# A fourth chunk of x turned by VectorE and carried inside SBUF, V's tiles moved by 32 bytes, the last products in fresh banks, four reciprocals put two instructions later

## The chip, the core and the metric

The kernel runs on one core of one Trainium2 chip. The metric is the device time of one execution in microseconds; the time given for the kernel before is the median of 3 runs. Beside the runs there is one profiled execution, whose rows are quoted below. The engines are called as in the profile: PE (TensorE, matrix products), DVE (VectorE), ACT (ScalarE), POOL (GpSimd) and SP (SyncE, which here only issues transfers).

## What is computed

One layer of an encoder trunk on x of 512 tokens by 2048, in float32:

```python
h = rms_norm(x, norm_w)
q, k, v, g_attn, xr, g_lru = jnp.split(h @ w_in, SPLITS, axis=-1)    # widths 1024 256 256 1024 1024 1024
attn_out = attention_group(q, k, v, q_norm_w, k_norm_w)              # 8 heads, 2 key heads, full softmax
lru_out = lru_group(xr, conv_w, conv_b, lru_wa, ...)                 # conv of 4 taps, gated linear scan both ways
mixed = concat([rms_norm(attn_out, attn_norm_w) * silu(g_attn),
                rms_norm(lru_out, lru_norm_w) * silu(g_lru)])
return x + mixed @ w_out                                             # w_out: 2048 by 2048
```

## The kernel before

Every float32 operand of a product is split into a high part (rounded to the PE's float32r format, a cast on ACT) and a low part (the rest, a subtraction on DVE), and each product is done as three: high by high, high by low, low by high. PE thus runs 2755 products, nearly all of 128 stationary columns by 512 moving columns, in an order written out by hand.

**The first stage.** x comes in eight chunks x0 to x7 of 256 columns, one transfer of 512 KB each; `w_in`'s rows come in matching chunks w0 to w7 (`wraw`), and are split by `wsplit` (L218 the cast on ACT, L219 the subtraction on DVE that gives `wl`). The first projection (`proj_feat`, products in L388 and L153 to L155) needs chunk c of x with its columns on the partitions, so x must be turned. Chunks 0 to `TURNED`-1 = 4 are turned on PE: `xturn` runs two times four transposes of 128x128 (L253), after which ACT scales the result by the norm's weight and DVE forms the low part. Chunks 5, 6 and 7 are turned on DVE: `blocks` (L281) transposes 32x32 blocks in place of the whole, `put_aside` (L289) writes the tile to DRAM in one transfer of 512 KB, and `bring_back` (L296) reads it in four transfers of 128 KB that put the blocks where they belong; then ACT scales (L338) and casts (L339) and DVE subtracts (L339). The sums of squares for the norm are formed by `xsquare`, on DVE for the chunks below `TURNED` (L272) and on ACT for the others (L268); their sum (`xsum`, L373) feeds `rstd` on POOL (L346, L347) and two diagonal tiles on DVE (L357 to L360).

The order of these steps is a table, `moves`: after output e of chunk c, the entry (c, e) names the steps that are written next: `x5` is the next step of chunk 5, `w5` the load and `s5` the split of w5. SP's order in this stage is the order written. Each of SP's transfers signals one of eight semaphores in turn, and in the program it waits until the transfer eight places before it has landed. ACT and DVE follow the written order at the start and, from (1, 2) on, an order by priorities that is fixed when the program is built.

**Attention.** `kv` splits the values into `vh` and `vl`, tiles `v` that `values` uses as stationary operand (32 times three products `mm<-ph,v`, `mm<-pl,v`). They are made by `aside`, which takes a tile 64 bytes longer and uses it from byte 32 on. In the built program each of these tiles begins at a multiple of 64 bytes, as the other operands of the products do, so V's data begins at 32 past such a multiple.

**The group norm of the attention.** While the last projection (`C_GA + SEQ`) runs, `later` sums the squares and `spread` gives 1/rms: ACT's square root (L832) and four reciprocals of 128x128 on DVE (L835), whose place among DVE's other work the priorities set.

**The end.** The output product is done with sums of row blocks of `w_out` (seven products in place of eight). In the last group three accumulations are left, and each takes the row pairs i = 6 and 7 at the very end; `last` adds the accumulator (s = 0 and 1 of 128 tokens each) to the output tile on DVE (L1066) and sends it out (L1058). For the last of all, s = 1 is added and sent in two halves of 256 columns.

Of the kernel before, what the change touches and what calls it, by code (L numbers as in the profile page):

```python
# [51 lines left out]
B = 32  # L52
TURNED = 5
NQ = P // B
# [9 lines left out]
def hybrid_kernel(  # L64
# [166 lines left out]
    ssq = const([P, NT, KT // 2], "ssq")  # L231
    highs, x_parts, squared = {}, [], []

# [15 lines left out]
    def xturn(xc, kk, then=None):  # L249
        pt = mm()  # L250
        for t in range(NT):
            ks = slice(kk % 2 * P, (kk % 2 + 1) * P)
            nc.tensor.transpose(pt[:, t * P : (t + 1) * P], xc[:, t, ks], ident)  # L253
# [7 lines left out]
        nc.vector.scalar_tensor_tensor(  # L261
            xl[kk], pt, nw[:, kk : kk + 1], f(xh[kk]), op0=ALU.mult, op1=ALU.subtract
        )

    def xsquare(xc, c):
        for t in range(NT):
            if c >= TURNED:
# [3 lines left out]
                continue  # L271
            square = nc.vector.scalar_tensor_tensor(  # L272
                xc[:, t, :], xc[:, t, :], 1.0, xc[:, t, :], op0=ALU.mult, op1=ALU.mult,
                accum_out=ssq[:, t, c : c + 1],
            )
            if c == 1:
                squared.append(square.ins)

# [13 lines left out]
    def bring_back(to, aside_):  # L292

        src = aside_.rearrange("(i c) b x -> b c i x", c=B)
        for b in range(NQ):
            nc.sync.dma_start(  # L296
                to[b * B : (b + 1) * B].rearrange("p i k t r -> p i (k t r)"), src[b]
            )

    def in_order(v):  # L300
        return v.rearrange("p (t i r) -> p i t r", t=NT, i=NQ)

    def xchunk(c):
# [27 lines left out]
        yield  # L331
        with tc.high_priority(AHEAD), behind(split_done[-1]):
            for k in range(2):
# [4 lines left out]
                nc.scalar.activation(v, v, AF.Identity, scale=nw[:, kk : kk + 1])  # L338
                x_parts[:] = nc.scalar.copy(hi, v).ins, nc.vector.tensor_sub(lo, v, f(hi)).ins  # L339
        yield  # L340

# [312 lines left out]
    def kv(es):  # L654
# [3 lines left out]
        for t in range(NT):  # L658
            vv = es[t][:, NKV * HD :]
            vt = aside(  # L660
                lambda *a: pools["qkv"].tile(*a, tag="v", bufs=NT, name=nm("v")), 2 * NKV * HD // H
            )
            vh[t], vl[t] = vt[:, 0, :], vt[:, 1, :]
# [162 lines left out]

    def spread(dst, parts, n):

# [4 lines left out]
        for t in range(NT):  # L833
            ts_ = slice(t * P, (t + 1) * P)
            nc.vector.reciprocal(dst[:, ts_], dst[:, ts_])  # L835

# [14 lines left out]
    def seven(pair, hi, lo):  # L851
# [11 lines left out]
    def aside(tile_of, n):  # L863

        t = tile_of([P, n * H + 16], F32R)
        return t[:, 8 : 8 + n * H].rearrange("p (n e) -> p n e", e=H)

# [146 lines left out]
    def outputs(work):  # L1014
# [13 lines left out]

        def product(dst, i, k, b, n):
            ah, al = (t[:, k] for t in mixed[i][1])  # L1030
            bh, bl = (t[:, n] for t in b)
            for s in range(2):
                ts_ = slice(s * P, (s + 1) * P)
                for j, (lh, rh) in enumerate(((ah, bh), (ah, bl), (al, bh))):
                    nc.tensor.matmul(  # L1035
                        dst[s], lh[:, ts_], rh, start=i == 0 and j == 0, stop=i == 7 and j == 2
                    )
# [11 lines left out]
        for g in range(2):  # L1049
# [9 lines left out]

            def last(t0, j, acc, cut=1):  # L1060
                for s in range(2):
                    n = cut if s else 1
                    for e0 in range(0, SEQ, SEQ // n):
                        e1 = e0 + SEQ // n
                        to = xs[j][:, t0 + s, e0:e1]
                        nc.vector.tensor_add(to, to, acc[s][:, e0:e1])  # L1066
                        queue = nc.scalar if e1 < SEQ else nc.sync
                        leave(t0 + s, j, queue if g else nc.gpsimd, e0, e1)

# [118 lines left out]
    def split_x(c):  # L1188
# [3 lines left out]
    moves = {  # L1192
# [158 lines left out]
    def later():  # L1351
# [3 lines left out]
        with tc.high_priority():  # L1355
            spread(gbc, parts, NH * HD)
        yield 4
# [88 lines left out]
```

## Time and profile before

| | |
|---|---|
| runs | 630.40, 630.35, 630.19 us; median 630.35 |
| profiled execution | 630.3 us, of which the span of its instructions is 628.2 |
| granted TensorE clock | 0.999 |
| busy | PE 622.0 us, DVE 494.6, ACT 353.1, POOL 101.4 |
| transfers | 127.61 MB, mean 203 GB/s |

Starts are in microseconds from the span's start. A row of the timeline gives start, time taken, engine, line, operation, output<-inputs, shape, the count of instructions put together, and in brackets the idle time of the engine before it and what ended it. A product's row lasts longer than the distance to the next product, since products are pipelined: the pace is read from starts. The chain of work that ended last gives start, share of the time and what it was spent on. A row of transfers gives their number, size and the median time from issue to landing.

### The profile page before, as it was taken

The numbers are of one execution on the slowest core, as the hardware profiler recorded it, in microseconds if no ns is written. First come the engines' busy times: TensorE is split into PE (matmuls) and PEld (weight loads), VectorE is DVE, ScalarE is ACT, GpSimd is POOL, SyncE is SP. The second block draws the span as 40 slices with busy tenths as digits, with TensorE's granted clock in tenths as the row PEclk, the third lists the DMA queues.
The fourth block names the chain that finished last, engine by engine and source line by source line (L and its number), as shares of the span: only waits on it lengthen the run. The fifth ranks groups of instructions, "written<-read, shape, count | busy, mean of one in ns | idle before, by whom it ended". The sixth has DMA issues, their size and how long they took to land.

```text
span 628.2 us, 8273 instructions
## 1 busy us (share of the span) xinstructions
PE 622.0 (99%) x2755; PEld 512.5 (82%) x2755; DVE 494.6 (79%) x794; ACT 353.1 (56%) x618; POOL 101.4 (16%) x134
## 2 busy tenths in 40 slices
PE   9999999999999999999999999999999999999997
PEld 7888888888888888888888888887888888888885
DVE  5958979986699875987887888549978866886885
ACT  3674899379946823555475447438436643444441
POOL 0000210112002622522122232100120101110010
PEclk9999999999999999999999999999999999999999
DMA  8878785859774599479668646922996777896252
GB/s 284 281 209 263 176 202 172 176 134 192 237 234 135 172 255 227 109 214 267 183 170 254 194 150 185 268 69 67 280 232 204 224 254 244 287 340 213 68 201 100
DMA packets 73594, 127.61 MB, mean 203 GB/s; under 512 B 6616, under 2 KB 29264, under 8 KB 73552
## 3 DMA queue, kind: packets, MB, share of 16 engines
q1 hardware_dynamic: 65664, 109.65, 55.9%
q0 software_dynamic: 7712, 17.31, 14.2%
q8 instruction: 21, 0.34, 0.2%
q14 instruction: 21, 0.17, 0.1%
q10 hardware_dynamic: 176, 0.14, 0.1%
HBM read 110.29 MB, written 37.75 MB: 236 GB/s over the span
## 4 chain that ended last, share of the span: by engine, by line
PE 98%; DVE 1%; issue 0%; DVEq 0%; POOL 0%; POOLq 0%
PE pj L155 20%; PE pj L153 20%; PE pj L154 20%; PE mm L1035 14%; PE pj L1035 10%; PE mm L155 4%; PE mm L153 3%; PE mm L154 3%; PE pj L388 1%; PE mm L253 1%; PE mm L1153 1%; DVE gbc L835 1%; DVE wl L219 0%; DVE cb L1066 0%; PE mm L831 0%
## 5 line engine op out<-in xcount | busy, mean ns | idle before, releaser
L155 PE MATMUL pj<-x,wl 128*128 128x512 f32 x376 | 146.8, 390 | 0.4 <-DVE wl L219 0.3
L153 PE MATMUL pj<-x,wh 128*128 128x512 f32 x376 | 147.0, 391 | 0.0
L154 PE MATMUL pj<-x,wh 128*128 128x512 f32 x376 | 146.6, 390 | 0.0
L218 ACT CAST wh<-wr 128x512 fp32r<-128x512 f32 x143 | 85.4, 617 | 81.9 <-PE pj L154 32.0
L219 DVE TENSOR_TENSOR wl<-wr,wh 128x512 fp32r<-128x512 f32 x144 | 100.0, 724 | 21.2 <-ACT wh L218 19.9
L887 ACT CAST wh<-wr 128x1024 fp32r<-128x1024 f32 (+1 forms) x72 | 60.5, 860 | 77.3 <-PE mm L1035 35.9
L888 DVE TENSOR_TENSOR wl<-wr,wh 128x1024 fp32r<-128x1024 f32 (+1 forms) x72 | 68.5, 985 | 30.7 <-ACT wh L887 30.5
L155 PEld LDWEIGHTS pj<-x,wl 128*128 128x128 f32 x376 | 70.6, 188 | 16.1 <-DVE wl L219 1.3
L153 PEld LDWEIGHTS pj<-x,wh 128*128 128x128 f32 x376 | 70.6, 188 | 14.7
L154 PEld LDWEIGHTS pj<-x,wh 128*128 128x128 f32 x376 | 70.6, 188 | 14.7
L153 PE MATMUL pj<-wh,x 128*128 128x512 f32 x192 | 74.8, 389 | 0.0
L155 PE MATMUL pj<-wh,x 128*128 128x512 f32 x192 | 74.8, 389 | 0.0
L154 PE MATMUL pj<-wl,x 128*128 128x512 f32 x192 | 74.8, 389 | 0.0
L911 POOL DMA_DIRECT2D t<-in_w_out_dram x40 | 33.5, 901 | 161.3 <-DMA t<-in_w_out_dram 99.5
L1035 PE MATMUL mm<-wl,mh 128*128 128x512 f32 x128 | 49.8, 389 | 0.0
L1035 PE MATMUL mm<-wh,mh 128*128 128x512 f32 x128 | 49.8, 389 | 0.0
L1035 PE MATMUL mm<-wh,ml 128*128 128x512 f32 x128 | 49.8, 389 | 0.0
L153 PEld LDWEIGHTS pj<-wh,x 128*128 128x128 f32 x192 | 36.0, 188 | 7.5
L154 PEld LDWEIGHTS pj<-wl,x 128*128 128x128 f32 x192 | 36.0, 188 | 7.5
L155 PEld LDWEIGHTS pj<-wh,x 128*128 128x128 f32 x192 | 36.0, 188 | 7.4
L708 POOL TENSOR_SCALAR p<-p,sm 128x512 f32<-128x512 f32 x32 | 24.3, 764 | 90.0 <-DVE sm L707 90.0
L1035 PE MATMUL pj<-wh,mh 128*128 128x512 f32 x96 | 37.4, 390 | 0.0
(200 smaller groups left out, 1038.2 us busy)
## 6 DMA issues: line engine op xcount, KB each, us to landing
wr<-in_w_in_dram SPq DMA_DIRECT2D x71, 512.0 KB, 5.1
wr<-in_w_out_dram SPq DMA_DIRECT2D x24, 512.0 KB, 5.1
t<-in_w_out_dram POOLq DMA_DIRECT2D x40, 256.0 KB, 6.8
wr<-t SPq DMA_DIRECT2D x40, 256.0 KB, 5.9
pd<-u SPq DMA_DIRECT2D x16, 512.0 KB, 3.0
pt<-pd SPq DMA_DIRECT2D x64, 128.0 KB, 3.9
t<-in_w_out_dram SPq DMA_DIRECT2D x24, 256.0 KB, 5.5
t<-t SPq DMA_DIRECT2D x16, 256.0 KB, 5.7
```

Of the source, the lines that this page charges most:

```text
L153: nc.tensor.matmul(acc, lh, rh, start=start, stop=False)
L154: nc.tensor.matmul(acc, lh, rl, start=False, stop=False)
L155: nc.tensor.matmul(acc, ll, rh, start=False, stop=stop)
L218: copy(hi, raw[:, k, :]).ins,
L219: nc.vector.tensor_sub(lo, raw[:, k, :], f(hi)).ins,
L253: nc.tensor.transpose(pt[:, t * P : (t + 1) * P], xc[:, t, ks], ident)
L388: nc.tensor.matmul(acc[e], w[:, e * P : (e + 1) * P], x_[k], start=k == 0 and j == 0, stop=False,)
L708: last_pool[0] = nc.gpsimd.tensor_scalar(p, p, sm, 0.0, op0=ALU.mult, op1=ALU.add).ins
L887: nc.scalar.copy(hi[:, to], b)
L888: nc.vector.tensor_sub(lo[:, to], b, f(hi[:, to]))
L911: nc.gpsimd.dma_start(dst, src, accum_op=ALU.add)
L1035: nc.tensor.matmul(dst[s], lh[:, ts_], rh, start=i == 0 and j == 0, stop=i == 7 and j == 2)
```

## The change

Four things change.

1. `TURNED` goes from 5 to 4, so that chunk 4 is also turned by DVE, and `put_aside` and `bring_back` give way to `carry`: twelve transfers of 32 KB from SBUF to SBUF per chunk on SP, and four copies of 32x256 on POOL for the blocks that stay on their partitions. The table `moves` and the places of the squares change with it: the squares of chunk 5 now follow chunk 4's cast on ACT, and those of chunks 6 and 7 follow chunk 5's.
2. V's tiles are plain tiles, 64 bytes shorter, with the data at their start. In the built program they begin at multiples of 64.
3. The last accumulation (`Q4`): s = 1 is closed after i = 5 and added to the output then; i = 6 and 7 run for s = 0 first and then for s = 1 in two halves of 256 columns, each in a bank of its own.
4. The four reciprocals of the attention's norm are put behind the two subtractions that end the split of the chunk in work.

```diff
-TURNED = 5
+TURNED = 4
@@ in the first stage
+    def carry(to, u):
+
+        def at_(v, b):
+            return v[b * B : (b + 1) * B]
+
+        for d in range(1, NQ):
+            for b in range(NQ):
+                i = (b + d) % NQ
+                nc.sync.dma_start(at_(to, b)[:, i], at_(u, i)[:, b])
+        for b in range(NQ):
+            nc.gpsimd.tensor_copy(at_(to, b)[:, b], at_(u, b)[:, b])
...
-        with tc.high_priority(AHEAD), tc.issue_after(squared[-1] if c == TURNED else split_done[3][1]):
+        raw_x[c] = xc
+        with tc.high_priority(AHEAD), behind(lows_of(c)):
             for t in range(NT):
                 blocks(u, t, xc[:, t, :])
         yield
         with tc.high_priority(AHEAD):
-            there = put_aside(u, "xd", KT // 2 - TURNED)
-        with tc.issue_after(highs[TURNED - 1]):
-            xsquare(xc, c)
-        yield
-        with tc.high_priority(AHEAD):
-            bring_back(back, there)
+            carry(back, u)
+        if c == TURNED:
+            with tc.issue_after(highs[c - 1]):
+                xsquare(xc, c)
...
+        for n in {4: (5,), 5: (6, 7)}.get(c, ()):
+            with behind(x_parts[:1]):
+                xsquare(raw_x[n], n)
@@ moves
-        (2, 0): "x5 x4 x5", (2, 1): "x4 w3", (2, 2): "x6 x7", (2, 3): "w4 s3",
+        (2, 0): "x6 x4", (2, 1): "x5 w4", (2, 2): "x7 x5", (2, 3): "s3 x4",
...
@@ V
-            vt = aside(
-                lambda *a: pools["qkv"].tile(*a, tag="v", bufs=NT, name=nm("v")), 2 * NKV * HD // H
-            )
+            vt = pools["qkv"].tile([P, 2, NKV * HD], F32R, tag="v", bufs=NT, name=nm("v"))
@@ spread
-    def spread(dst, parts, n):
+    def spread(dst, parts, n, those=()):
...
-            nc.vector.reciprocal(dst[:, ts_], dst[:, ts_])
+            with behind(those):
+                nc.vector.reciprocal(dst[:, ts_], dst[:, ts_])
...
-            spread(gbc, parts, NH * HD)
+            spread(gbc, parts, NH * HD, split_done[turn_of[0] - 2][1:])
@@ the end
-                    product(dst, i, k, parts[u][b], n)
+                    if g and i == NP - 3 and k == Q4:
+                        product(dst, i, k, parts[u][b], n, (0,))
+                        product(dst, i, k, parts[u][b], n, (1,), ends_=(0, i))
+                        nc.vector.tensor_add(xs[j][:, t0 + 1], xs[j][:, t0 + 1], dst[1])
+                    else:
+                        product(dst, i, k, parts[u][b], n)
...
-            for i in (NP - 2, NP - 1):
-                product(dst, i, k, parts[24 + i][b], n)
-            last(t0, j, dst, 2 if k == Q4 else 1)
+            pieces = [(dst, (0, 1), 0, SEQ, (0, NP - 1))]
+            if k == Q4:
+                pieces = [(dst, (0,), 0, SEQ, (0, NP - 1))] + [
+                    ((None, pj()), (1,), e0, e0 + H, (NP - 2, NP - 1)) for e0 in (0, H)
+                ]
+            for to, ss, e0, e1, ends_ in pieces:
+                for i in (NP - 2, NP - 1):
+                    product(to, i, k, parts[24 + i][b], n, ss, slice(e0, e1), ends_)
+                last(t0, j, to, ss, e0, e1)
```

On SP, in the first stage, the order before begins here with the load of x6, the thirteenth transfer. `b` is a chunk of x, `wr` a chunk of `w_in`, `xu` a turned chunk and `xd` its place in DRAM.

```order
L240 DMA b_61_378<-in_x_dram 128x4x256
L240 DMA b_62_380<-in_x_dram 128x4x256
L206 DMA wr_388<-in_w_in_dram 128x2x512
L289 DMA xd_404<-xu_336 128x1024
L206 DMA wr_410<-in_w_in_dram 128x2x512
L296 DMA xu_337<-xd_404 32x4x256 x4
L206 DMA wr_416<-in_w_in_dram 128x2x512
L289 DMA xd_436<-xu_424 128x1024
L289 DMA xd_442<-xu_430 128x1024
L296 DMA xu_425<-xd_436 32x4x256 x4
L206 DMA wr_488<-in_w_in_dram 128x2x512
L296 DMA xu_431<-xd_442 32x4x256 x4
```

The order now, from the same thirteenth transfer on (x6), to the load of w7.

```order
L240 DMA b_55_344<-in_x_dram 128x4x256
L306 DMA xu_258<-xu_257 32x256 x12
L206 DMA wr_378<-in_w_in_dram 128x2x512
L240 DMA b_59_386<-in_x_dram 128x4x256
L306 DMA xu_373<-xu_372 32x256 x12
L206 DMA wr_444<-in_w_in_dram 128x2x512
L206 DMA wr_446<-in_w_in_dram 128x2x512
L306 DMA xu_439<-xu_438 32x256 x12
L306 DMA xu_455<-xu_454 32x256 x12
L206 DMA wr_536<-in_w_in_dram 128x2x512
```

The fifteen transfers that moved three chunks are now forty-eight that move four; w4 and x7 stand behind the twelve of chunk 4, w5 and w6 behind those of chunk 5, and w7 behind those of chunks 6 and 7.

On ACT, the order before from chunk 5's scale (`xu_337`) to chunk 6's casts (`xu_425`); `b_62` is x7, whose squares it forms, and `wh` the high parts of w5.

```order
L338 ACTIVATE xu_337<-xu_337,nw 128x4x128 x2
L339 CAST x_81_468<-xu_337 128x4x4x32
L268 ACTIVATE b_62_380,ssq<-b_62_380 128x256
L339 CAST x_83_473<-xu_337 128x4x4x32
L218 CAST wh_519<-wr_410 128x512
L218 CAST wh_523<-wr_410 128x512
L268 ACTIVATE b_62_380,ssq<-b_62_380 128x256 x3
L338 ACTIVATE xu_425<-xu_425,nw 128x4x128 x2
L339 CAST x_90_527<-xu_425 128x4x4x32
L339 CAST x_92_532<-xu_425 128x4x4x32
```

The same stretch now: `xu_373` is chunk 5, `xu_439` chunk 6, `b_55` x6 and `b_59` x7.

```order
L352 ACTIVATE xu_373<-xu_373,nw 128x4x128 x2
L353 CAST x_78_512<-xu_373 128x4x4x32
L353 CAST x_80_517<-xu_373 128x4x4x32
L218 CAST wh_563<-wr_444 128x512
L218 CAST wh_567<-wr_444 128x512
L268 ACTIVATE b_55_344,ssq<-b_55_344 128x256 x4
L268 ACTIVATE b_59_386,ssq<-b_59_386 128x256 x4
L352 ACTIVATE xu_439<-xu_439,nw 128x4x128 x2
L353 CAST x_87_571<-xu_439 128x4x4x32
L353 CAST x_89_576<-xu_439 128x4x4x32
```

All eight squares of x6 and x7 now stand between w5's split and chunk 6, where four of x7's stood around w5's split. On DVE the sum over all squares and what follows from it (L373 to L360 before) stand ahead of chunk 6's subtractions, before and now.

On DVE, at the reciprocals of the attention's norm, before:

```order
L861 TENSOR_TENSOR ml_4272<-hs_1448,mh_4271 128x768
L835 RECIPROCAL gbc<-gbc 128x128 x4
L219 TENSOR_TENSOR wl_4219<-wr_4216,wh_4218 128x512
L219 TENSOR_TENSOR wl_4223<-wr_4216,wh_4222 128x512
L219 TENSOR_TENSOR wl_4328<-wr_4325,wh_4327 128x512
L219 TENSOR_TENSOR wl_4332<-wr_4325,wh_4331 128x512
```

And now:

```order
L877 TENSOR_TENSOR ml_4316<-hs_1492,mh_4315 128x768
L219 TENSOR_TENSOR wl_4263<-wr_4260,wh_4262 128x512
L219 TENSOR_TENSOR wl_4267<-wr_4260,wh_4266 128x512
L851 RECIPROCAL gbc<-gbc 128x128 x4
L219 TENSOR_TENSOR wl_4372<-wr_4369,wh_4371 128x512
L219 TENSOR_TENSOR wl_4376<-wr_4369,wh_4375 128x512
```

The first pair of low parts passes ahead of the four reciprocals; the second pair stays behind them.

More of the change, by code (lines that the diff above doesn't have):

```diff
@@ L231, in hybrid_kernel @@
     ssq = const([P, NT, KT // 2], "ssq")
-    highs, x_parts, squared = {}, [], []
+    highs, lows, x_parts = {}, {}, []
     def xload(c, nk=1):
@@ L260, in xturn @@
             ).ins
-        nc.vector.scalar_tensor_tensor(
+        lows[kk // 2] = nc.vector.scalar_tensor_tensor(
             xl[kk], pt, nw[:, kk : kk + 1], f(xh[kk]), op0=ALU.mult, op1=ALU.subtract
-        )
+        ).ins
     def xsquare(xc, c):
@@ L271, in xsquare @@
                 continue
-            square = nc.vector.scalar_tensor_tensor(
+            nc.vector.scalar_tensor_tensor(
                 xc[:, t, :], xc[:, t, :], 1.0, xc[:, t, :], op0=ALU.mult, op1=ALU.mult,
@@ L275, in xsquare @@
             )
-            if c == 1:
-                squared.append(square.ins)
     def blocks(u, t, src):
@@ L298, in bring_back, with lows_of @@
             )
+    def carry(to, u):
[7 more added lines that the diff above has]
+            nc.gpsimd.tensor_copy(at_(to, b)[:, b], at_(u, b)[:, b])
     def in_order(v):
         return v.rearrange("p (t i r) -> p i t r", t=NT, i=NQ)
+    raw_x = {}
+    def lows_of(c):
+        return {4: (), 5: (lows.get(2),), 6: split_done.get(3), 7: split_done.get(3)}[c][-1:]
     def xchunk(c):
@@ L659, in kv @@
             vv = es[t][:, NKV * HD :]
-            vt = aside(
-                lambda *a: pools["qkv"].tile(*a, tag="v", bufs=NT, name=nm("v")), 2 * NKV * HD // H
-            )
+            vt = pools["qkv"].tile([P, 2, NKV * HD], F32R, tag="v", bufs=NT, name=nm("v"))
             vh[t], vl[t] = vt[:, 0, :], vt[:, 1, :]
@@ L861, in seven @@
             nc.vector.tensor_sub(lo[:, to], part, f(hi[:, to]))
-    def aside(tile_of, n):
-        t = tile_of([P, n * H + 16], F32R)
-        return t[:, 8 : 8 + n * H].rearrange("p (n e) -> p n e", e=H)
     def kept(pool, i):
@@ L1027, in feed, with product @@
                 next(feeds[u])
-        def product(dst, i, k, b, n):
+        def product(dst, i, k, b, n, ss=range(2), es=slice(None), ends_=(0, NP - 1)):
             ah, al = (t[:, k] for t in mixed[i][1])
             bh, bl = (t[:, n] for t in b)
-            for s in range(2):
+            for s in ss:
                 ts_ = slice(s * P, (s + 1) * P)
@@ L1035, in product @@
                     nc.tensor.matmul(
-                        dst[s], lh[:, ts_], rh, start=i == 0 and j == 0, stop=i == 7 and j == 2
+                        dst[s][:, es], lh[:, ts_], rh[:, es],
+                        start=i == ends_[0] and j == 0, stop=i == ends_[1] and j == 2,
                     )
@@ L1058, in leave, with last @@
                 queue.dma_start(of[tokens[t], c0 + e0 : c0 + e1], xs[j][:, t, e0:e1])
[L1060 to L1068, printed above, removed]
+            def last(t0, j, acc, ss=range(2), e0=0, e1=SEQ):
+                for s in ss:
+                    to = xs[j][:, t0 + s, e0:e1]
+                    nc.vector.tensor_add(to, to, acc[s][:, e0:e1])
+                    queue = nc.scalar if e1 < SEQ else nc.sync
+                    leave(t0 + s, j, queue if g else nc.gpsimd, e0, e1)
             p1, q5, q6, q7 = banks(*((mm, mm, pj, pj), (pj, mm, mm, pj))[g])
```

8 rows, old and new, of the table moves are left out of this document.

## The prediction

> **What bounds the kernel.** I read the page's busy times first, then PE's groups, then the chain of work that ended last, and from there the timeline at the few places where PE loses time.
>
> ```profile
> span 628.2 us, 8273 instructions
> PE 622.0 (99%) x2755; PEld 512.5 (82%) x2755; DVE 494.6 (79%) x794; ACT 353.1 (56%) x618; POOL 101.4 (16%) x134
> L155 PE MATMUL pj<-x,wl 128*128 128x512 f32 x376 | 146.8, 390 | 0.4 <-DVE wl L219 0.3
> ...
> 471.21 2.72 PE mm L1035 x12
> ```
>
> PE is busy throughout, and its costliest groups wait for next to nothing. In the chain twelve products take 2.72 us, so the pace is 0.227 us a product. An edit can gain only by taking work off PE, ending one of its few waits, a better pace, or less behind its last product; it loses wherever PE is made to wait. The profiled execution took 630.3 us, 2.1 of them outside the span; the median of the runs is 630.35, and I add the sum to that. A difference below 0.2%, 1.26 us, is about what cannot be told from none.
>
> **Chunk 4's transposes.**
>
> ```profile
> 23.16 0.87 PE mm L253 x8
> ...
> 42.94 0.40 PE L153 MATMUL pj<-x,wh 128*128 128x512 f32 x1
> 43.17 0.39 PE L154 MATMUL pj<-x,wh 128*128 128x512 f32 x1
> 43.66 0.50 PE L155 MATMUL pj<-x,wl 128*128 128x512 f32 x1
> 44.00 0.40 PE L153 MATMUL pj<-x,wh 128*128 128x512 f32 x1
> ```
>
> Without the eight transposes PE comes 0.87 us earlier to all that follows. That is a gain only if nothing waits there. Before, one product waits: chunk 6's third, the first that takes low weights, starts at 43.66 where 43.17 + 0.23 = 43.40 was due (the next one, 0.34 behind it, loses another 0.11). With 24 products, 5.4 us, to a chunk it is now due at 42.53. So when is chunk 6 ready? The prices:
>
> ```profile
> 11.41 2.53 SPq L240 DMA_DIRECT2D b<-in_x_dram  x2
> 34.79 1.74 SPq L296 DMA_DIRECT2D xu<-xd  x4
> 39.48 0.36 SPq L180 DMA_DIRECT2D vec_st<-in_conv_b_dram  x1
> 39.88 0.32 SPq L180 DMA_DIRECT2D vec_st<-in_lru_ba_dram  x1
> ...
> b<-in_x_dram SPq DMA_DIRECT2D x1, 512.0 KB, 9.2
> wr<-in_w_in_dram SPq DMA_DIRECT2D x1, 512.0 KB, 3.8
> vec_st<-in_lru_lambda_dram SPq DMA_DIRECT2D x1, 8.0 KB, 2.1
> pd<-u SPq DMA_DIRECT2D x16, 512.0 KB, 3.0
> xu<-xd SPq DMA_DIRECT2D x5, 128.0 KB, 5.4
> wr<-in_w_in_dram SPq DMA_DIRECT2D x71, 512.0 KB, 5.1
> ...
> 18.00:20.00 2.00, 2.00 (x13) 1.69 (x12) 2.00 (x4) 1.55 (x4) 0.00 (x0) 1.00 1.08 353
> ```
>
> The first four are issues on SP: four small transfers in 1.74, 0.44 each, or 0.40 at the shortest (39.48 to 39.88); I take 0.45. Behind them are landings: x6 is issued at 11.41 and lands 9.2 later, at 20.6; a chunk of weights lands 3.8 behind its issue on a nearly empty queue, 5.1 in the median. The last row is the full queue at 353 GB/s, so that 512 KB take 1.5.
>
> No transfer of 32 KB from SBUF to SBUF is in the trace. Its landing lies between the 2.1 of the smallest load and the 3.0 of the 512 KB that leave SBUF; 5.4 is a small one behind other work. I take 2.1, the nearest in size, and keep 3.0.
>
> SP walks its queue like this. The twelve transfers of chunk 4 are its 14th to 25th; the 21st waits for x6, the 13th, at 20.6. Five issues later, at 22.85, w4 goes; it lands at 26.65, and x7 behind it at 28.1. Chunk 5's are the 28th to 39th, and the 35th waits for x7, the 27th. The 39th goes at 28.1 + 4 x 0.45 = 29.9 and lands at 32.0. From there ACT and DVE go on as they do before for chunk 6, with the eight squares in between:
>
> ```profile
> 35.47 0.40 ACT L268 ACTIVATE b<-b 128x256 f32<-128x256 f32 x1
> 39.83 1.34 ACT L338 ACTIVATE xu<-xu,nw 128x512 f32<-128x512 f32 x2 [3.87 <-DMA xu<-xd]
> 42.10 1.14 ACT L218 CAST wh<-wr 128x512 fp32r<-128x512 f32 x2
> ...
> 36.00 0.19 DVE L373 TENSOR_REDUCE xsum<-ssq 128x4 f32<-128x32 f32 x1 [0.35 <-ACT b L268]
> 37.92 1.29 DVE L360 TENSOR_TENSOR k<-ident,part 128x512 fp32r<-128x512 f32 x2
> 41.71 1.29 DVE L339 TENSOR_TENSOR x<-xu,x 128x512 fp32r<-128x512 f32 x2 [2.50 <-ACT x L339]
> 42.92 1.29 DVE L219 TENSOR_TENSOR wl<-wr,wh 128x512 fp32r<-128x512 f32 x2
> ```
>
> From a chunk's scale to the end of its weights' casts ACT takes 39.83 to 43.24, 3.4. Eight squares at 0.40 follow, the last starting 7 x 0.40 later, and the sum over them 36.00 - 35.47 = 0.53 after that. So the sum starts at 32.0 + 3.4 + 2.8 + 0.53 = 38.7. From the sum to the end of the two diagonal tiles is 36.00 to 39.21, 3.2: 41.9. Only then does DVE come to chunk 6's subtractions, and from the first of these to the product that needs the low weights is 41.71 to 43.66, 1.95. The product starts at 43.85.
>
> Before it was 43.66. So the 0.87 is spent in a longer wait at the same product (1.3 in place of 0.26) and 0.2 beyond it is lost: the term is +0.2. With issues at 0.40 and x7 0.3 earlier it is -0.5; with landings of 3.0 and w4 taking the median 5.1 it is +2.4. The other chunks have more room. Chunk 5's low weights are ready at 32.0 + 43.66 - 39.83 = 35.8, due at 37.1. Chunk 7's transfers follow w6, which lands at 35.6, with 16 issues: 42.8, landed 44.9, ready 48.7, due one chunk behind 43.85, at 49.4.
>
> Chunk 6's own transfers end earlier in that row, landed at 39.6, which alone would have it ready at 43.4.
>
> Work at no cost: DVE gets chunk 4's four transposes of 32x32 blocks and gives its four squares to ACT, which forms them while it waits for the transfers; without that wait they would cost it 4 x 0.40 = 1.6. POOL's copies have a bound in the next row: 764 ns for twice the columns on 128 partitions, so at most 3.1 us for four, while the twelve transfers beside them need 5.4 to issue. If that cover failed, chunk 5's chain would begin later by the rest.
>
> ```profile
> L708 POOL TENSOR_SCALAR p<-p,sm 128x512 f32<-128x512 f32 x32 | 24.3, 764 | 90.0 <-DVE sm L707 90.0
> ...
> 316.76 0.39 PE L153 MATMUL mm<-kt,q 128*128 128x512 f32 x1
> 317.45 0.39 PE L153 MATMUL mm<-ph,v 128*128 128x512 f32 x1
> 320.01 0.39 PE L155 MATMUL mm<-ph,v 128*128 128x512 f32 x1
> 320.24 0.40 PE L153 MATMUL pj<-x,wh 128*128 128x512 f32 x1
> ```
>
> **V's tiles.** Twelve products with V go from 317.45 to 320.24, 0.2325 each, against 0.227; three with K, ahead of them, 0.23 each, the slow one being that into V's first load. There are 96 products with V: 96 x 0.006 = 0.6 us. V is the one stationary operand that begins at 32 past a multiple of 64, so I take -0.6; the ends are 0 and -0.6. The Trainium skill, "SBUF — State Buffer", Specifications, has lines of 16 bytes and a price for each new line; by that a shift of 32 bytes changes nothing and the sum is 0.6 higher. No row here shows V at another place, so that stays a rival.
>
> **The reciprocals.**
>
> ```profile
> 432.24 1.13 ACT L218 CAST wh<-wr 128x512 fp32r<-128x512 f32 x2
> 434.71 3.39 DVE L835 RECIPROCAL gbc<-gbc 128x128 f32<-128x128 f32 x4
> 438.01 2.43 DVE L219 TENSOR_TENSOR wl<-wr,wh 128x512 fp32r<-128x512 f32 x4
> ...
> 437.98 0.39 PE L154 MATMUL pj<-x,wh 128*128 128x512 f32 x1
> 438.70 0.50 PE L155 MATMUL pj<-x,wl 128*128 128x512 f32 x1 [0.33 <-DVE wl L219]
> 439.04 0.40 PE L153 MATMUL pj<-x,wh 128*128 128x512 f32 x1
> ```
>
> The casts are done at 433.4, but the subtractions stand behind 3.3 us of reciprocals, and PE loses 0.72 - 0.23 = 0.49 and, at the next product, 0.34 - 0.23 = 0.11. With the first pair ahead, it runs from 434.7 to 435.9, due 438.2: -0.6, all of it. The reciprocals end at 439.2 in place of 438.0, which is when the second pair begins now (four in 2.43 from 438.01), so what is queued behind them on DVE is not later. Ends: -0.6, and -0.3 if a later wait takes half.
>
> **The end.**
>
> ```profile
> 622.92 1.43 DVE L1066 TENSOR_TENSOR cb<-cb,mm 128x512 f32<-128x512 f32 x3 [1.35 <-PE mm L1035]
> 623.63 1.08 SPq L1058 DMA_DIRECT2D out_dram<-cb  x2
> ```
>
> After PE's last product DVE adds two halves, and SP's last issue, the second of the two, starts at about 624.4. Now only one half is left: about a quarter of 1.43 less, -0.35. Against it, twelve products of 256 columns replace six of 512. At half price they cost nothing more; the transposes, 0.87 for eight with a stationary load each, show 0.11 possible, half of 0.227; at the full 0.227 they would cost 1.4. I take 0.01 each, +0.1: -0.25.
>
> **Sum**: +0.2 - 0.6 - 0.6 - 0.25 = -1.25, hence 630.35 - 1.25 = 629.1.
>
> **The rivals.** (a) The queue is quicker: issues at 0.40, x7 earlier, term -0.5, 628.4. For it speaks that 32 KB is less to describe than the 128 KB that gave 0.44; against it the many waits for landings. (b) V's pace stays: 629.7, no change to be told. Against it: the slow step out of the products with K is the one into V's load. The 16-byte lines of the Trainium skill would make it so. (c) Slower: a small transfer lands after 5.4 us. With eight on the way at a time issues are then 5.4/8 = 0.68 apart; the five ahead of w4 and the four behind x7 add 9 x 0.23 = 2.1 and the landing 3.3, so chunk 5 is there at 37.4, and chunk 6's third product comes 5.4 later than reckoned: 634.5. It decides from where the chain is 2.5 us later than reckoned, chunk 5 landed at 34.5. Against it: the queue has little else in it after 24 us.
>
> **Chances.** The sum as reckoned 0.45, (a) 0.25, (b) 0.18, (c) 0.10; 0.02 for anything else. The sum lies on the bound of 1.26, so its chance is halved: faster 0.22 + 0.25 = 0.47, the same 0.23 + 0.18 + 0.02 = 0.43, slower 0.10. The range takes in (a) and (b) and the weights' median landing with part of its price: 628.1 to 630.4.
>
> **What would show it.** The transposes in PE's row near 23 are gone; chunk 6's third product starts at 43.3 to 44.3, released by DVE, behind a sum that starts at 38 to 39.5. Products with V go at 0.227. No wait on `wl` near 437. SP's last issue comes 0.5 us or less behind PE's last product's end. The forecast is wrong if chunk 6 or 7 waits for a landing, if the low weights of chunk 6 are ready by 42.6, or if V's pace does not move.

## The result, and the profile after

The changed kernel takes 636.21 us in the median of five runs (635.66 to 637.6), against 630.35 before: a ratio of 1.010 with a 95% interval of 1.0086 to 1.0113. It is slower by about 5.9 us, outside the predicted range of 628.1 to 630.4. The profiled execution took 637.6, with a span of 635.8, so it is the slowest of the five.

From the page of the kernel after: its span, the granted clock in 40 slices, and two of PE's groups.

```profile
span 635.8 us, 8350 instructions
...
PEclk9997999999999999999999999999999999999999
...
L153 PE MATMUL pj<-x,wh 128*128 128x512 f32 x376 | 148.2, 394 | 4.6 <-ACT wh L218 4.6
L155 PE MATMUL pj<-x,wl 128*128 128x512 f32 x376 | 147.7, 393 | 1.4 <-DVE wl L219 1.4
```

The first of these groups, in the kernel before:

```profile
L153 PE MATMUL pj<-x,wh 128*128 128x512 f32 x376 | 147.0, 391 | 0.0
```

The group that waited for nothing now has 4.6 us of idle time ahead of it, that of the low weights 1.4 instead of 0.4, and the clock falls in the fourth slice, 48 to 64 us. So the first stage comes next. PE's timeline of the kernel after:

```profile
31.75 0.39 PE L154 MATMUL pj<-x,wh 128*128 128x512 f32 x1
33.51 0.50 PE L155 MATMUL pj<-x,wl 128*128 128x512 f32 x1 [1.37 <-DVE wl L219]
...
45.04 0.39 PE L155 MATMUL pj<-x,wl 128*128 128x512 f32 x1
47.75 0.80 PE L153 MATMUL pj<-x,wh 128*128 128x512 f32 x1 [2.32 <-ACT wh L218]
48.34 0.63 PE L154 MATMUL pj<-x,wh 128*128 128x512 f32 x1
48.77 0.66 PE L155 MATMUL pj<-x,wl 128*128 128x512 f32 x1
...
54.64 0.39 PE L155 MATMUL pj<-x,wl 128*128 128x512 f32 x1
56.85 0.50 PE L153 MATMUL pj<-x,wh 128*128 128x512 f32 x1 [1.82 <-ACT wh L218]
...
62.07 0.48 PE L153 MATMUL pj<-x,wh 128*128 128x512 f32 x1
```

Starts that should be 0.227 apart are 1.76 apart at chunk 4's third product, 2.71 at chunk 6's first and 2.21 at chunk 7's first. Behind the last two the products go 0.427 apart instead of 0.227 for some 3.4 us. Two stretches of the kernel after show both (columns: sum, busy time and instructions of PE, of its weight loads, of DVE, ACT and POOL, then granted clock, DMA share and GB/s):

```profile
40.00:50.00 10.00, 7.68 (x28) 5.71 (x28) 4.88 (x11) 6.48 (x22) 1.24 (x2) 0.88 0.22 54
50.00:60.00 10.00, 8.18 (x28) 5.96 (x27) 2.58 (x4) 3.50 (x6) 0.00 (x0) 0.84 0.53 149
```

In ten microseconds PE runs 28 products instead of 44, at a granted clock of 0.88 and 0.84, and the DMA engines are busy for 0.22 of the first stretch, at 54 GB/s. The same stretch before:

```profile
40.00:50.00 10.00, 9.90 (x44) 7.86 (x43) 4.99 (x8) 8.41 (x15) 0.00 (x0) 1.00 0.81 202
```

So the data are late while the DMA engines have little to do. SP's queue in the kernel after says why:

```profile
16.65 8.36 SPq L306 DMA_DIRECT2D xu<-xu  x12
25.11 0.53 SPq L206 DMA_DIRECT2D wr<-in_w_in_dram  x1
25.68 0.47 SPq L240 DMA_DIRECT2D b<-in_x_dram  x1
26.25 8.25 SPq L306 DMA_DIRECT2D xu<-xu  x12
34.59 1.04 SPq L206 DMA_DIRECT2D wr<-in_w_in_dram  x2
35.73 16.22 SPq L306 DMA_DIRECT2D xu<-xu  x24
52.06 0.52 SPq L206 DMA_DIRECT2D wr<-in_w_in_dram  x1
```

SP issues with hardly a pause from 16.65 to 52: it stands 0.8 us for an earlier load at 18.6, 0.8 for x7 at 30.7 and 0.2 for w6 at 40.0, and its last issue takes 1.6. The 48 issues take 0.59 us each in the median; six that wait for nothing take 3.76, so they start 0.63 apart. Chunk 7's issues end at 51.95, and only then can w7 be loaded, at 52.06.

Where PE's time went, by the starts of products less the pace of 0.227: 0.4 more at the start (the clock comes up to full at 6.67 us instead of 5.76; in the profiles of all kernels here that moment lies between 4.3 and 7.1, so this is not the change's), 2.8 in waits for chunks 4 and 5 (31.7 to 41), 2.5 at chunk 6, 1.7 in slow products behind it, 2.0 at chunk 7, 2.0 in slow products behind that. Less the 0.87 of the transposes and the 0.35 that was lost at chunk 6 before, this makes 10.2; the product that starts at 62.07 here starts at 52.01 before, 10.06 earlier. From there on the other three parts win 2.5 back, and the span is 7.6 longer.

### The profile page after: what moved, and what is told of

Same layout as the page of the kernel before. It is cut to its first block, busy times and chain, and to the rows that moved or that the text cites. A ratio compares the mean times of both kernels' runs of the same rounds, so it can differ in the third digit from the quotient of the medians.

```text
span 635.8 us, 8350 instructions
## 1 busy us (share of the span) xinstructions
PE 624.9 (98%) x2753; PEld 514.0 (81%) x2753; DVE 496.1 (78%) x791; ACT 355.8 (56%) x628; POOL 109.5 (17%) x150
## 4 chain that ended last, share of the span: by engine, by line
PE 90%; SPq 4%; DMA 3%; DVE 1%; issue 0%; ACT 0%; ACTq 0%
PE pj L155 19%; PE pj L153 19%; PE pj L154 19%; PE mm L1046 13%; PE pj L1046 10%; PE mm L155 3%; PE mm L154 3%; PE mm L153 3%; SPq L306 3%; DMA wr<-in_w_in_dram 3%; DMA b<-in_x_dram 1%; SPq L206 0%; DVE x L261 0%; DVE b L272 0%; DVE xu L279 0%
## 5 line engine op out<-in xcount | busy, mean ns | idle before, releaser
L1046 PE MATMUL pj<-wl,mh 128*128 128x512 f32 (+1 forms) x100 | 38.5, 385 | 0.0
```

What stands on the lines that cost most here:

```text
L1046: nc.tensor.matmul(dst[s][:, es], lh[:, ts_], rh[:, es], start=i == ends_[0] and j == 0, stop=i == ends_[1] and j == 2,)
```

## The experiments

No experiment leaves out a part of the computation; the dummies and the measurements come on top of it.

### The parts apart

The first kernel has parts 2 to 4 of the change (V's tiles, the end, the reciprocals) and the first stage of before; the second has part 1 alone.

```diff
@@ parts 2 to 4, from the kernel after
-TURNED = 4
+TURNED = 5
...
-            carry(back, u)
+            there = put_aside(u, "xd", KT // 2 - TURNED)
@@ part 1, from the kernel after
-            vt = pools["qkv"].tile([P, 2, NKV * HD], F32R, tag="v", bufs=NT, name=nm("v"))
+            vt = aside(
...
-            spread(gbc, parts, NH * HD, split_done[turn_of[0] - 2][1:])
+            spread(gbc, parts, NH * HD)
```

> The kernel before with V's tiles, the reciprocals and the end of the change, but its own first stage. The theory (the loss is all in the first stage, the other three parts do what was reckoned): V's pace 0.6, the wait near 437 gone 0.6, the end 0.2 to 0.4, so 630.35 - 1.4 to 1.6 = 628.8 to 629.0, faster by 0.2 to 0.25%. The rival (what the three parts win is lost again elsewhere, or the loss lies in one of them): 630 or more.

> The kernel before with the first stage of the change alone. The theory: the loss of the whole change plus the 1.4 to 1.6 that the other parts win, 636.2 + 1.5 = 637.7, with PE's waits for chunks 4 to 7 as in the changed kernel, and the granted clock at half behind the two longest. The rival (the parts do not add up): nearer to 636 or 639.

Parts 2 to 4 alone: 627.40 us (627.19 to 627.68), ratio 0.9958 (0.9945 to 0.9970), faster than both kernels. Part 1 alone: 637.82 (636.67 to 639.86), ratio 1.0133 (1.0118 to 1.0149); its profile has the waits for chunks 4 and 6 and the slow products behind the latter. Against 630.1 for the kernel before, measured beside them, that is -2.7 and +7.7, together 5.0, near to the 5.9 measured. The loss is all in the first stage. The three parts win more than reckoned. Of the kernel with them alone, PE at the first products with V and near 437, PE's last product, and SP's last four issues:

```profile
316.77 0.39 PE L153 MATMUL mm<-ph,v 128*128 128x512 f32 x1
...
317.90 0.39 PE L155 MATMUL mm<-ph,v 128*128 128x512 f32 x1
...
437.84 0.39 PE L154 MATMUL pj<-x,wh 128*128 128x512 f32 x1
438.06 0.39 PE L155 MATMUL pj<-x,wl 128*128 128x512 f32 x1
...
621.20 0.28 PE L1029 MATMUL pj<-wh,ml 128*128 128x256 f32 x1
...
618.77 3.54 SPq L1053 DMA_DIRECT2D out_dram<-cb  x4
```

Five steps with V take 1.13, 0.226 each. Between 270 and 420 us PE was 0.9 above its pace before and is at it now. Near 437 nothing waits (0.66 won). SP's last issue ends at 622.31, 1.11 behind the start of PE's last product; before, the last product started at 623.17, and SP's last four issues were these, in the timeline of the kernel before:

```profile
620.91 3.80 SPq L1058 DMA_DIRECT2D out_dram<-cb  x4
```

Their end at 624.71 is 1.54 behind that start, so 0.43 is won there, and the span ends 3.0 behind the last issue instead of 3.5: 0.5 more. Less 0.08, since twelve half products take 1.44 against six whole ones' 1.36, the end is worth 0.85. The kernel after has the same end: the span ends 4.1 behind the start of PE's last product in both, 5.0 before. In this kernel's profile chunk 6's third product also does not wait; the code there is that of before, so that 0.35 varies from run to run.

### Half of the transfers on another queue

The kernel after, with every second transfer of `carry` issued by POOL.

```diff
-                nc.sync.dma_start(at_(to, b)[:, i], at_(u, i)[:, b])
+                queue = nc.gpsimd if b % 2 else nc.sync
+                queue.dma_start(at_(to, b)[:, i], at_(u, i)[:, b])
```

> The changed kernel with half of each chunk's twelve transfers issued by POOL instead of SP. The theory (SP's queue is what is late: 48 issues at 0.63 us each): 24 issues, 15 us, leave SP's queue; on POOL six issues at about 0.9 make 5.4 us a chunk, so that four chunks are through by about 41 in place of 52 us; chunks 6 and 7 no longer make PE wait, the clock stays up behind them, and 2.5 + 2.0 + 3.6 = 8.1 us come back: 628 to 630. The rival (the transfers themselves land late, whoever issues them): the waits stay, 635 to 637.

632.73 us (630.47 to 633.6, ten runs), ratio 1.0035 (1.0025 to 1.0046). The transfers' kind, number and size are the same; only who issues them differs, and 3.5 of the 5.9 us come back. All have landed by about 38 us instead of 53. PE's rows in the profile of this kernel:

```profile
42.83 0.40 PE L154 MATMUL pj<-x,wh 128*128 128x512 f32 x1
44.73 0.50 PE L155 MATMUL pj<-x,wl 128*128 128x512 f32 x1 [1.50 <-DVE wl L219]
...
45.30 0.40 PE L154 MATMUL pj<-x,wh 128*128 128x512 f32 x1
46.61 0.49 PE L155 MATMUL pj<-x,wl 128*128 128x512 f32 x1 [0.91 <-DVE wl L219]
```

The waits for chunks 4, 5 and 7 are gone, as is the slow clock in this execution. It is the fastest of the ten: it and the next have a mean clock of 0.999 and 1.0, the eight others, 631.7 and more, one of 0.993 to 0.997, so those still have slow products that no profile shows. What was not expected is the new wait at chunk 6's third product, for low weights. The Trainium skill, "DMA: Bandwidth & Descriptors", Rules for kernel authors, says that spreading transfers over several engines' queues brings no bandwidth and only saves the issuing sequencer's time. No run here measures that bandwidth by itself; the time of the issues is what the trace shows, and here it was what counted.

### The sum put later

In the last kernel DVE takes the diagonal tiles ahead of chunk 6's low weights, and stands for POOL's root first. Here that step follows chunk 6's low weights.

```diff
-        if (c, e) in ((4, 3), (KT // 2 - 1, 0)):
+        if (c, e) in ((5, 3), (KT // 2 - 1, 0)):
             with tc.high_priority(AHEAD), tc.issue_after(split_done[-1][1]):
                 next(stats)
```

> The kernel with half of the transfers on POOL's queue, and the sum of the squares with what follows it (POOL's reciprocal root, DVE's diagonal tiles) put behind chunk 6's low weights instead of ahead of them. There chunk 6's third product waits 1.67 us and a later one 1.08 for low weights. The theory (DVE, in order, stands for POOL's root with the low weights behind it, as the prediction had it): both waits go, 2.7 us, 632.7 - 2.7 = 630.0. The rival (chunk 6 itself is late): the waits stay, 632 to 633.

627.72 us (627.67 to 628.38), ratio 0.9965 (0.9951 to 0.9979): 5.0 less than the kernel ahead in the median, 2.8 between the two profiled spans (628.4 and 625.6), and its runs lie within 0.7 us of each other, at a clock of 0.999 to 1.0. Both waits are gone. What is left in PE's timeline of this kernel is small:

```profile
41.73 0.39 PE L155 MATMUL pj<-x,wl 128*128 128x512 f32 x1
42.49 0.50 PE L153 MATMUL pj<-x,wh 128*128 128x512 f32 x1 [0.37 <-ACT wh L218]
```

So the chain that the prediction followed, sum, root, tiles, low weights, is real, and was hidden in the kernel after by x being later still. With both repaired the first stage costs what it did before: 627.72 stands beside the 627.40 with the old first stage. The 0.87 of the transposes is spent again, at chunk 6.

### POOL's copies first, and POOL's work in turn

Chunk 6 now waits for POOL's four copies, which stand behind the issues of chunk 7. Two attempts at that, both from the kernel with the sum put later: the copies ahead of a chunk's own issues; and POOL's issues held until the copies of the chunk ahead are done.

```diff
@@ the copies first
+        for b in range(NQ):
+            nc.gpsimd.tensor_copy(at_(to, b)[:, b], at_(u, b)[:, b])
         for d in range(1, NQ):
...
-        for b in range(NQ):
-            nc.gpsimd.tensor_copy(at_(to, b)[:, b], at_(u, b)[:, b])
@@ in turn
-                queue.dma_start(at_(to, b)[:, i], at_(u, i)[:, b])
+                with behind(copied if b % 2 else ()):
+                    queue.dma_start(at_(to, b)[:, i], at_(u, i)[:, b])
         for b in range(NQ):
-            nc.gpsimd.tensor_copy(at_(to, b)[:, b], at_(u, b)[:, b])
+            copied[:] = [nc.gpsimd.tensor_copy(at_(to, b)[:, b], at_(u, b)[:, b]).ins]
```

> The last kernel with POOL's four copies of a chunk ahead of its six issues instead of behind them. Chunk 6 now waits for the copies from 36.9, where its transfers have landed, to 39.1. The theory: it is ready 2 us earlier, nothing waits on PE between 20 and 62 us, and the 0.87 of chunk 4's transposes are at last a gain over the 627.4 of the kernel with the other three parts alone: 626.5. The rival (POOL's issues, now 1.7 us later per chunk, make the transfers late instead): 629 or more.

> The kernel with half of the transfers on POOL and the sum put later, with POOL's six issues of a chunk held behind the copies of the chunk ahead of it, so that chunk 6's copies do not stand behind chunk 7's issues. The theory: chunk 6 is ready at about 37 instead of 39.1, the last wait in the first stage (0.53 + 0.24 + 0.11 + some small ones at chunk 6, 1.2 in all) goes, and chunk 4's transposes are a gain at last: 627.7 - 1.2 = 626.5. The rival (chunk 7, whose transfers now leave POOL 2 to 3 us later, waits instead): 627.5 to 629.

Both missed, and the rival of each came. The first took 633.01 (631.27 to 633.75), ratio 1.0043 (1.0028 to 1.0058): POOL's queue now alternates the issues of chunks 6 and 7, chunk 6's are late, and PE waits for it from 41.9 to 46.2, with slow products behind. The second took 628.63 (627.68 to 633.89, twelve runs), ratio 0.9991 (0.9971 to 1.001), no difference from the kernel before that can be told, and not below the 627.72 from which it started. Its wait has moved on by one chunk; DVE's rows in this second kernel show the same thing in front of chunk 7's low weights:

```profile
45.95 0.18 DVE L392 TENSOR_REDUCE xsum<-ssq 128x4 f32<-128x32 f32 x1
47.68 0.17 DVE L376 CAST part<-rstd 128x4 fp32r<-128x4 f32 x1 [1.55 <-POOL rstd L366]
...
49.17 1.28 DVE L219 TENSOR_TENSOR wl<-wr,wh 128x512 fp32r<-128x512 f32 x2
```

That the 0.87 can be won was not shown.

### By way of DRAM again

The kernel after with four chunks as now, but five transfers each by way of DRAM in place of twelve.

```diff
-            carry(back, u)
+            bring_back(back, put_aside(u, "xd", KT // 2 - TURNED))
```

> The changed kernel with chunks 4 to 7 turned by way of DRAM as before (one transfer out, four back) in place of twelve from SBUF to SBUF and four copies. The theory (SP's queue is what is late): a chunk takes 5 issues of 0.44 and one wait for the transfer out, 3.0, on SP, 5.2 in place of 7.6; the four are through some 9 us earlier, chunks 6 and 7 wait little and the clock stays up: 629 to 632. The rival (each hop's landing is what counts, and two hops are slower than one): the waits for chunks 5 to 7 stay or grow, 636 or more.

638.38 us (636.85 to 639.21), ratio 1.0127 (1.0108 to 1.0146). The number of issues alone does not make the queue quick. SP's rows in this kernel:

```profile
16.42 0.34 SPq L287 DMA_DIRECT2D xd<-xu  x1
23.20 1.88 SPq L294 DMA_DIRECT2D xu<-xd  x4
...
26.18 0.45 SPq L287 DMA_DIRECT2D xd<-xu  x1
32.84 1.75 SPq L294 DMA_DIRECT2D xu<-xd  x4
```

The transfer out lands behind loads of 512 KB, and SP, in order, stands for it from 16.8 to 23.2 and from 26.6 to 32.8, with everything behind it. I had reckoned 3.0 for that wait. The table `moves` of before puts the way out and the way back into different steps, with other issues in between.

### The waits filled

Products of no use stand where PE waits for chunks 6 and 7, so that it is busy.

```diff
+FILL = {(5, 3): 20, (6, 3): 16}
...
         move(step)
+        if step in FILL:
+            busy(FILL[step], mm())
```

> The changed kernel with 20 products of no use (256 columns of ones into a bank that nobody reads, about 0.11 us each) on PE ahead of chunk 6's products and 16 ahead of chunk 7's, where it waits 2.5 and 2.0 us. The theory (the halved clock behind the two waits comes of the waits): the dummies take 2.2 and 1.8 us of the waits, the products behind run at 0.227 and not 0.427, and 1.7 + 1.9 = 3.6 us come back: 632.6. The rival (the slow products have another cause, such as operands or transfers): they stay at 0.427 and the time at 636.

638.24 us (636.43 to 640.28), ratio 1.013 (1.0111 to 1.0149): not the 632.6 of the theory, and yet its mechanism is there. In the profile the products behind both waits run at full pace: the first starts at 47.56 (47.75 in the kernel after), and from 48.79 they are 0.23 apart. But the 1.7 won behind chunk 6 is lost in front of chunk 7, which is no sooner there; only the 1.7 behind chunk 7 remains at 60 us. Then a wait that the kernel after does not have takes it back, in PE's timeline of this kernel:

```profile
104.32 0.50 PE L154 MATMUL mm<-k,k 128*128 128x512 f32 x1 [1.84 <-ACT b L544]
...
105.73 0.63 PE L156 MATMUL mm<-k,k 128*128 128x512 f32 x1
```

ACT had stood 0.70 of that time for a load of `lru_wx`. Behind this wait the clock is halved again, for 3.4 us. So the slow products come of the waits, and shortening one wait is not worth its length where the next one is set by a transfer. This profile is the slowest of the four runs, though. The other three have a mean clock of 0.999 to 1.0, above the 0.994 to 0.997 of every run of the kernel after, and still take 636.4 to 638.5: the clock's loss was taken away and the time was not won. Where these three lose it, no profile shows.

### The prices by themselves

Behind the whole kernel before, SP, ACT and POOL issue transfers between two tiles in SBUF, and PE runs bursts with pauses.

```diff
+        for n, cols in ((32, 256), (32, 128), (32, 512), (16, 256), (64, 256), (P, 256), (P, 512)):
+            for to in tos:
+                nc.sync.dma_start(to[P - n :, :cols], a[:n, :cols])
...
+        for n in (1, 2, 3, 4) * 4:
+            pt = mm()
...
+            nc.vector.tensor_copy(step, pt)
+            for _ in range(n - 1):
+                nc.vector.tensor_copy(step, step)
```

> The kernel before, followed by measurements of their own: on SP, eight issues each from SBUF to SBUF of 32 partitions x 1 KB, 32 x 512 B, 32 x 2 KB, 16 x 1 KB, 64 x 1 KB, 128 x 1 KB and 128 x 2 KB, then eight of 32 x 1 KB on ACT's and eight on POOL's queue; and on PE sixteen bursts of 64 products with pauses of about 1.0, 1.6, 2.3 and 2.9 us in turn. The theory: 32 x 1 KB costs SP 0.59 (0.63 with its gap) with nothing else on the chip's queues either, and POOL less; pauses of 2 us and more, not those below 1.6, are followed by products at half the clock. The rivals: the 0.59 was company in the queues, and it is 0.44 or less here; the clock halves only behind pauses of 3 us and more, or behind none.

Rows of SP and of POOL: eight issues of 32 partitions x 2 KB, eight of 128 x 1 KB, and three on POOL of 32 x 1 KB.

```profile
635.72 5.02 SPq L1416 DMA_DIRECT2D to<-from  x8
...
652.00 5.10 SPq L1416 DMA_DIRECT2D to<-from  x8
...
668.16 1.52 POOL L1419 DMA_DIRECT2D to<-from  x3 [0.30 <-issue]
```

With 0.59 for the last, eight in 5.02 start 0.63 apart; eight of 128 partitions 0.64. The other shapes, 16 to 64 partitions and 512 B to 2 KB, are the same, but for two issues of the 56 that took 1.6 and 1.8. So the price is that of a transfer from SBUF to SBUF, whatever its size within these shapes, and not of company in the queue. On ACT it is 0.51 to 0.61 but for one of 0.76, on POOL 0.50. On SP those of 32 partitions land 1.8 to 2.0 us after the issue with little else under way. None of the sixteen pauses, the longest 2.44 between starts (2.2 of PE idle), halved the clock, against the theory. So a second kernel had longer ones, behind bursts of fp32r products and of bf16.

```diff
+        for kind in (1, 0):
+            for n in (2, 3, 4, 5, 6) * 4:
...
+                        nc.tensor.matmul(pt, wide[:, :P], wide, start=True, stop=True)
```

> The kernel before, followed by 20 bursts of 30 fp32r products like the kernel's own (512 columns, 6.8 us a burst), with pauses on PE of about 1.4, 1.9, 2.3, 2.8 and 3.3 us in turn, and then the same with bursts of 64 bf16 products of 256 columns. One theory: the kind of product counts; behind fp32r products pauses of 2 us and more halve the clock for 3.4 us, behind bf16 products they do not below 2.8. The rival: the kind does not count, and both behave alike, halved from some length on or at some phases only.

Five of its stretches: a pause of 2.2 us (652.18 to 654.35) and what followed it; a pause of 3.1 us (724.82 to 727.91), cut in two at 726.14, and what followed it (the clock stands third from the end):

```profile
651.05:654.46 3.41, 1.24 (x8) 0.80 (x6) 1.97 (x4) 0.00 (x0) 0.00 (x0) 1.00 0.00 0
654.46:657.88 3.42, 3.42 (x10) 2.65 (x10) 0.00 (x0) 0.00 (x0) 0.00 (x0) 0.50 0.00 0
722.73:726.14 3.41, 2.09 (x10) 1.49 (x9) 1.21 (x3) 0.00 (x0) 0.00 (x0) 1.00 0.00 0
726.14:729.56 3.42, 1.65 (x8) 1.39 (x8) 1.62 (x4) 0.00 (x0) 0.00 (x0) 1.00 0.00 0
729.56:732.97 3.41, 3.41 (x17) 2.83 (x16) 0.00 (x0) 0.00 (x0) 0.00 (x0) 1.00 0.00 0
```

The shorter pause halves the clock and the longer one does not. Over both kernels: of 28 pauses of 0.8 to 1.7 us idle none did; of 12 of 2.2, four; of 8 of 2.6, four; of 8 of 3.1, three. Both kinds of product do it, so the first theory falls, and the rival stands: from about 2 us on it is a matter of when the pause falls.

The traces say when. In the clock records of all twelve kernels here, every change lies a whole number of steps of 3.413 us behind the first rise of that execution, and the stretches above are five such steps. While the clock was full, 19 steps held 1.8 us or more of PE's idle time, and 18 of them were followed by a step at half clock (the nineteenth held 2.0); of 50 steps with 1.0 to 1.8 us, one was (1.6). The pause of 2.2 lies within one step; that of 3.1 is split by a step's end into 1.3 and 1.8 and goes free. In the kernel after, 2.20 of the 2.32 us ahead of chunk 6 and all 1.82 ahead of chunk 7 lie within one step. So a wait of 1.8 to 3 us halves the clock in some executions and not in others; the runs of the kernel after show it too: two at 637.2 and 637.6 have a mean clock of 0.994, the three at 635.7 to 636.2 one of 0.996 to 0.997.

## Why the prediction was wrong, point by point

**The step that failed is the price in the first term of the sum, chunk 4's transposes: an issue on SP, "I take 0.45".** It measured 0.59, 0.63 from start to start, and the term that was +0.2 came to +7.7 in the kernel with this part alone. I took it from four transfers of 128 KB out of DRAM as the nearest in size, and gave it an end below (0.40) and none above. The trace of before had a row nearer in kind, transfers whose two ends lie in the same memory, here DRAM:

```profile
L908 SPq DMA_DIRECT2D t<-in_w_out_dram x24: 491/504/598, 58.8 to 183.7; - x24
L908 SPq DMA_DIRECT2D t<-t x16: 469/547/985, 156.1 to 447.4; - x16
```

By the prediction's own walk, an upper end of 0.55 makes chunk 5 land 0.9 later (nine issues) and chunk 7's transfers another 1.6 (sixteen): enough to leave the range, though chunk 5 would not have reached the rival's 34.5. With the measured 0.63 the same walk gives 1.6 and 2.9 and a term of about +4, an estimate: the price alone is half of the +7.7, and the rest stands in the next four points.

**The walk to chunk 5's landing** kept its order but had no room for anything else. Chunk 5 landed at 35.8 in place of 32.0. Issues at 0.63 make 1.6 of these 3.8 us. Another 1.3 came before w4: SP stood 0.8 for an earlier load that the walk does not have, and with issues at 0.63 the wait for x6 that was to cover such delays no longer binds (x6 landed at 20.66, as reckoned, and the issue held for it went at 21.89). And x7 landed 6.3 behind w4's issue, where 5.3 was reckoned. ACT and DVE in the kernel after, at chunks 5, 6 and 7:

```profile
35.89 1.34 ACT L352 ACTIVATE xu<-xu,nw 128x512 f32<-128x512 f32 x2 [3.28 <-DMA xu<-xu]
...
44.81 1.34 ACT L352 ACTIVATE xu<-xu,nw 128x512 f32<-128x512 f32 x2 [1.74 <-POOL rstd L364]
...
53.34 1.34 ACT L352 ACTIVATE xu<-xu,nw 128x512 f32<-128x512 f32 x2 [5.12 <-DMA xu<-xu]
...
43.10 0.19 DVE L390 TENSOR_REDUCE xsum<-ssq 128x4 f32<-128x32 f32 x1 [2.44 <-ACT b L268]
```

**The chain behind it held in length, but was not what PE waited for.** From 35.89 on the prediction's own steps, 3.4, 2.8, 0.53, 3.2 and 1.95, give the sum at 42.6 and chunk 6's third product at 47.8; measured are 43.10 and 48.77, the latter already with the slow clock. But chunk 6's first product came no sooner than 47.75: its own transfers, set aside at 39.6 as early enough, landed at 44.55 at the soonest, and its scale starts at 44.81. (That row names POOL's root, which ended then by chance; in the program the scale waits for POOL's copies, done at 35.6, and for the transfers.) So ACT stood for a landing at chunk 6 and at chunk 7, which is the prediction's own sign of being wrong.

**Chunk 4** is not in the walk at all, and its third product waited. DVE, in order, stood 1.48 us for x7 (landed at 31.44) to turn chunk 7, with chunk 4's low weights, whose high parts were done by 31.0, behind that.

**Chunk 7** was reckoned ready at 48.7 and due at 49.4. Its products start at 56.85. The sixteen issues up to its last transfer began 4.6 later than reckoned, behind w6, and took 11.7 instead of 7.2; its scale starts at 53.34. The walk stopped there, but w7 stands behind them, was issued at 52.06, and PE's wait ended on its cast, for which ACT had stood another 0.47. A queue has to be walked to its last transfer that somebody waits for.

**The clock** is in no step. Slow products cost 3.7 of the 10.2 us in the profiled execution; the mean clock of the median run, 0.997 against 0.994, speaks for about half of that there, an estimate. The Trainium skill, "TensorE: Matmul & The Clock Gate", Why this matters for your kernels, names pauses above about 3 us as what to avoid; here waits of 1.8 and 2.3 idle were enough, where they fell within one step of 3.413 us, and the measurement decides.

**Landing** at 2.1: right, 1.9 in the median, though up to 5.0 behind loads of 512 KB. **POOL's copies at nothing**: right where SP alone issues, 0.45 each in the median, 2.0 a chunk beside 7.6 of issues; the cover was gone where POOL issued too. **PE's transposes**: gone, 0.87, and spent, as foreseen, with much more beside it.

**V's tiles**, -0.6: right; the pace is 0.227. It was worth 0.8 to 0.9, since the products next to those with V had been slower as well. A shift by 32 bytes thus counts, though by the lines of 16 bytes in the Trainium skill, "SBUF — State Buffer", Specifications, it should not; rival (b) falls. Only these two places were run, and the tiles became 64 bytes shorter along with the move. **The reciprocals**, -0.6: right, 0.66. **The end**, -0.25: right in kind, 0.85 in size; the last transfer's way out, 0.5 of it, was not in the step.

**Rival (c)**, 634.5, came nearest, by another way: it had issues 0.68 apart because landings were slow. The landings were quick and the issues themselves slow. Its point of decision, chunk 5 landed at 34.5, was passed by a little over 1 us, and its price lacked chunk 7 and the clock. Its 0.10 was too little for a term whose price no row showed.

## What to carry to other kernels

Price a DMA issue that the trace does not show by the row with the same kind of ends, not the same size, give it an end above, and multiply by the count on its queue: forty-eight times 0.18 is 8.6 us of SP's time, at 512 B and at 2 KB a partition alike. Walk the queue to the end, weights included; and where a wait in an in-order queue or engine goes, look for the next instruction that stands for something else. Of a change made of several parts, run the parts alone: three of these four make the fastest kernel measured here, 627.4.

## What the runs showed of the hardware

- An issue on SP from SBUF to SBUF takes 0.59 us for 16 to 128 partitions and 512 B to 2 KB each, one starting 0.63 to 0.64 behind the other; from DRAM to DRAM 0.50 to 0.55; most with one end in DRAM take 0.32 to 0.47. POOL issues the same transfer in 0.50. One of 32 partitions lands 1.8 to 2.0 us later when the queues are nearly empty.
- The granted clock changed only at whole steps of 3.413 us behind its first rise. A step with 1.8 us or more of PE's idle time was followed by one at half clock in 18 of 19 cases, one with 1.0 to 1.8 in 1 of 50; a pause of 3.1 us that a step's end divides can go free, and none of 1.7 and less ever halved it.
- A stationary operand of fp32r that begins at 32 past a multiple of 64 bytes cost 0.006 us a product, 0.6 for the 96 here, and 0.2 to 0.3 more on the products next to them.
